# Attention in steps of 32 queries of eight heads, score products of 16 queries by 144 keys, gates by tanh, all engines in written order

## The chip, the cores and the metric

The kernel runs on one core of one Trainium2 chip. The core has a matrix engine (TensorE, PE in the profile; its weight loads stand apart as PEld), three engines for elementwise work (VectorE or DVE, ScalarE or ACT, GpSimd or POOL), and DMA queues that are fed by SyncE (SP), ScalarE and GpSimd. The metric is the time of one execution on the device, in microseconds; lower is better. Three runs of the kernel before took 806.92 to 807.62 us, with a median of 807.46 us.

## The reference, cut to what matters

One layer of a transformer trunk for 512 tokens of width 2048: a sliding-window attention with 32 query heads in 4 groups that share a key and a value head, a gate, an output projection, and then a gated embedding and a last norm. Of these, the attention and its gate are what the change rewrites:

```python
hn = rmsnorm(x, norm_g[i])
q, k, v, gate = jnp.split(h @ w_in, [SWA_WIDTH, SWA_WIDTH + SWA_KV_WIDTH, SWA_WIDTH + 2 * SWA_KV_WIDTH], axis=-1)
...
scores = jnp.einsum('bnqhgd,bnjhd->bnhgqj', q, kb).astype(jnp.float32) * (SWA_HEAD_DIM ** -0.5) + bias
scores = jnp.where(mask, scores, jnp.finfo(jnp.float32).min)
m = jnp.maximum(scores.max(axis=-1, keepdims=True), sink)
e = jnp.exp(scores - m)
probs = e / (e.sum(axis=-1, keepdims=True) + jnp.exp(sink - m))
out = jnp.einsum('bnhgqj,bnjhd->bnqhgd', probs.astype(vb.dtype), vb).reshape(bsz, seq, SWA_WIDTH)
return (out * jax.nn.silu(gate)) @ w_out
```

A query sees itself and the 127 keys before it. The bias depends on the distance alone; each head has a sink that joins the sum but has no value. Everything is float32.

## The kernel before

Every float32 product of the projections is made of three products of split operands (`mm3`: high by high, low by high, high by low). An operand is split by a ScalarE copy to the high part and a VectorE subtraction to the low part. The input weights come in pieces of 128 x 1024 (`wraw`), which `Weights` splits into `whi` and `wlo`; a piece serves eight k-steps, and one k-step is three matmuls of 512 columns. Thirty chunks of 128 columns are projected with 16 k-steps each: 14 query chunks (a chunk is two heads, a pair) and 16 gate chunks. Two further query pairs, the keys and the values are projected in the first stage, up to about 72 us.

Attention is 64 steps. Step i belongs to `d`, a group of two query pairs (four heads), and `g`, a block of 64 queries. `scores(i)` makes two products, one for each pair: the queries of the block and the two heads are the 128 stationary columns, and the keys move, 128 (first two blocks) or 192, twice, for the high and the low part of the key: 256 or 384 moving columns. VectorE adds bias and both halves (L392), folds the two ends of the window on one another (L407), and takes the maximum (L409); ScalarE makes the exponentials with their sum (L412) and multiplies by the inverse sum (L415). GpSimd writes the sink beside the scores (L388). `turn(i)` transposes the shares on PE and splits them into `r`; for later blocks GpSimd selects (L437) the triangle that belongs to the window's own end into `own`, and ScalarE copies the low part of `own` to the other half of the partitions (L444). `weigh(i)` multiplies `r` by the values and `own` by a difference of values `DV`, and every second step adds the output's halves (L470, L471) into `U`.

The loop over steps emits `turn(i - 2)`, `weigh(i - 3)`, `scores(i)` and then seven k-steps of the projection, which fill PE. PE, SP and POOL run in the order written; VectorE and ScalarE are ordered by the framework's scheduler. When a query chunk is done `evac_q` splits it from PSUM; a gate chunk is multiplied by `rb` (the inverse norm), and a silu runs over four chunks at once (L490), then `gate_value` multiplies by `U` (L485). Between steps `sum_weights` prepares sums of weight blocks in DRAM: SP copies a block, and GpSimd adds another by a DMA that accumulates (L536). These sums serve the two later stages, the output projection and the gated embedding, which multiply in seven products of blocks instead of eight. Their weights are split like the input's (L565, L566, `bhi` and `blo`).

The PSUM pool `p` has two banks for the projections, the scores have one buffer of two banks, the transposes (`t`) and the weighed outputs (`o`) two banks each.

## Time and profile before

| what | value |
|---|---|
| median of three runs | 807.46 us |
| span of the profiled execution | 805.0 us |
| PE busy | 791.9 us, 98% of the span |
| DVE busy | 583.7 us, 73% |
| ACT busy | 508.2 us, 63% |
| POOL busy | 111.1 us, 14% |
| mean granted clock of PE | 0.996 |
| first and last score product | 83.58 us and 442.78 us |

The profile is of one execution. Its page gives the span of the program's instructions; what lies around the span isn't profiled, and the page has no other time for that execution. PE's busy time counts pipelined matmuls, so it tells that PE rarely stood still, and the distance between starts tells what a matmul costs. An idle time names the engine and the line that ended it.

### The profile page before, as it was taken

To read this page: it belongs to the slowest core of one execution; us is meant where nothing else is said; L and a number is where in the kernel's file an instruction comes from. 1 tells how busy PE (TensorE), PEld (TensorE's weight loads), DVE (VectorE), ACT (ScalarE), POOL (GpSimd) and SP (SyncE) were. 2 spreads that over 40 slices of the span, in tenths; PEclk is the share of its full clock that TensorE was granted. 3 is DMA by queue.
4 is the path that set the end of the run, shared out by engine and by line. 5 is a ranking of instruction groups with operands and counts; after the bars stand their busy time and mean duration, and the time that the engine had idled before them with its cause. 6 is when DMAs were issued, how large, how long until landed. Compare 5 with 4: busy or idle time off the path is not lost.

```text
span 805.0 us, 10943 instructions
## 1 busy us (share of the span) xinstructions
PE 791.9 (98%) x3760; PEld 661.4 (82%) x3760; DVE 583.7 (73%) x953; ACT 508.2 (63%) x1036; POOL 111.1 (14%) x219
## 2 busy tenths in 40 slices
PE   9999999999999999999999999999999999999995
PEld 8888888878888888888888888888888888878884
DVE  4537776777767787776777898766646977879686
ACT  5635566676667786666586754555568756757545
POOL 0003113122121313122121100030000020200000
PEclk9999999999999999999999999999999999999998
DMA  8862877768697877867685459899612996876533
GB/s 336 310 173 52 250 241 197 221 185 230 149 259 209 198 230 189 223 182 218 178 210 141 120 215 356 307 293 249 201 53 85 376 204 202 167 199 206 181 106 105
DMA packets 45255, 165.15 MB, mean 205 GB/s; under 512 B 5952, under 2 KB 8128, under 8 KB 41360
## 3 DMA queue, kind: packets, MB, share of 16 engines
q1 hardware_dynamic: 38080, 130.20, 47.8%
q0 software_dynamic: 6832, 33.88, 22.6%
q8 instruction: 29, 0.48, 0.2%
q10 hardware_dynamic: 288, 0.39, 0.1%
q14 instruction: 26, 0.21, 0.1%
HBM read 158.63 MB, written 46.19 MB: 254 GB/s over the span
## 4 chain that ended last, share of the span: by engine, by line
PE 86%; issue 7%; DVE 2%; DMA 2%; POOL 1%; ACT 1%; SPq 0%; DVEq 0%; POOLq 0%; ACTq 0%
PE qps L122 7%; PE qps L121 7%; PE qps L120 7%; PE gps L121 7%; PE gps L122 7%; PE gps L120 7%; PE o L121 6%; PE o L120 6%; PE o L122 6%; PE s L383 2%; PE g L121 2%; PE g L122 2%; PE g L120 2%; PE o L461 2%; PE vps L229 2%
## 5 line engine op out<-in xcount | busy, mean ns | idle before, releaser
L566 DVE TENSOR_TENSOR blo<-braw,bhi 128x1024 fp32r<-128x1024 f32 x80 | 97.8, 1222 | 42.5 <-ACT bhi L565 42.4
L565 ACT CAST bhi<-braw 128x1024 fp32r<-128x1024 f32 x80 | 84.1, 1051 | 58.1 <-PE g L122 15.9
L122 PE MATMUL gps<-xh,wlo 128*128 128x512 f32 x256 | 100.1, 391 | 0.0
L121 PE MATMUL gps<-xl,whi 128*128 128x512 f32 x256 | 100.1, 391 | 0.0
L120 PE MATMUL gps<-xh,whi 128*128 128x512 f32 x256 | 99.9, 390 | 0.2 <-DVE q L266 0.2
L107 DVE TENSOR_TENSOR wlo<-wraw,whi 128x1024 fp32r<-128x1024 f32 x60 | 73.3, 1222 | 23.6 <-ACT whi L106 21.1
L122 PE MATMUL qps<-xh,wlo 128*128 128x512 f32 x224 | 87.8, 392 | 0.0
L121 PE MATMUL qps<-xl,whi 128*128 128x512 f32 x224 | 87.7, 391 | 0.0
L120 PE MATMUL o<-bhi,fho 128*128 128x512 f32 x224 | 87.7, 391 | 0.0
L122 PE MATMUL o<-bhi,flo 128*128 128x512 f32 x224 | 87.2, 389 | 0.0
L121 PE MATMUL o<-blo,fho 128*128 128x512 f32 x224 | 87.2, 389 | 0.0
L120 PE MATMUL qps<-xh,whi 128*128 128x512 f32 x224 | 87.2, 389 | 0.0
L412 ACT ACTIVATE t<-t,sm 128x129 f32<-128x129 f32 x128 | 50.6, 397 | 45.7 <-DVE sm L409 45.6
L106 ACT CAST whi<-wraw 128x1024 fp32r<-128x1024 f32 x60 | 62.9, 1048 | 24.8 <-PE gps L121 9.0
L121 PE MATMUL g<-blo,fhg 128*128 128x512 f32 x192 | 74.9, 390 | 0.6 <-DVE blo L566 0.6
L120 PE MATMUL g<-bhi,fhg 128*128 128x512 f32 x192 | 75.1, 391 | 0.0
L122 PE MATMUL g<-bhi,flg 128*128 128x512 f32 x192 | 74.8, 389 | 0.0
L437 POOL TENSOR_SCALAR_AFFINE_SELECT own<-r 64x512 fp32r<-64x512 f32 (+1 forms) x48 | 33.2, 691 | 298.2 <-DVE r L428 289.4
L122 PEld LDWEIGHTS gps<-xh,wlo 128*128 128x128 f32 x256 | 48.1, 188 | 10.2
L120 PEld LDWEIGHTS gps<-xh,whi 128*128 128x128 f32 x256 | 48.1, 188 | 9.4 <-PE vps L229 0.4
L121 PEld LDWEIGHTS gps<-xl,whi 128*128 128x128 f32 x256 | 48.1, 188 | 8.9
L566 DVE TENSOR_TENSOR blo<-grown,bhi 128x1024 fp32r<-128x1024 f32 x32 | 39.1, 1222 | 17.1 <-ACT bhi L565 17.1
(201 smaller groups left out, 1699.9 us busy)
## 6 DMA issues: line engine op xcount, KB each, us to landing
wraw<-in_w_gate_in SPq DMA_DIRECT2D x32, 512.0 KB, 5.7
wraw<-in_w_q SPq DMA_DIRECT2D x28, 512.0 KB, 4.6
w_out<-in_w_out POOLq DMA_DIRECT2D x24, 512.0 KB, 7.4
braw<-in_w_out SPq DMA_DIRECT2D x24, 512.0 KB, 4.1
braw<-in_ple_gate SPq DMA_DIRECT2D x24, 512.0 KB, 4.3
w_out<-in_w_out SPq DMA_DIRECT2D x16, 512.0 KB, 6.0
ple_gate<-in_ple_gate SPq DMA_DIRECT2D x16, 512.0 KB, 5.6
ple_gate<-in_ple_gate POOLq DMA_DIRECT2D x16, 512.0 KB, 7.1
```

What stands on the lines that cost most here:

```text
L106: nc.scalar.copy(hi, raw)
L107: nc.vector.tensor_sub(lo, raw, hi.bitcast(F32))
L120: nc.tensor.matmul(ps, sh, mh, start=first, stop=False, skip_group_check=more)
L121: nc.tensor.matmul(ps, sh, ml, start=False, stop=False, skip_group_check=more)
L122: nc.tensor.matmul(ps, sl, mh, start=False, stop=last, skip_group_check=more)
L229: nc.tensor.matmul(v_ps[t], h[:, c], both[:, :, 256:512], start=f, stop=e, skip_group_check=True)
L383: nc.tensor.matmul(s_ps[:, u, : 2 * n], st, key[:, :, first : first + n], start=True, stop=True)
L412: nc.scalar.activation(su, su, AF.Exp, bias=sm[:, u : u + 1], accum_out=sm[:, 2 + u : 3 + u])
L437: nc.gpsimd.affine_select(out=flat(own), in_=flat(r).bitcast(F32), pattern=[[0, 8], [sign, HB]], compare_op=ALU.is_ge, fill=0.0, base=-HB ...
L461: nc.tensor.matmul(out, first, r[:, low], start=low == 0, stop=own is None and low == 1)
L565: nc.scalar.copy(hi, raw)
L566: nc.vector.tensor_sub(lo, raw, hi.bitcast(F32))
```

## The change

Attention is cut in another way. A step now belongs to `kv`, a group of eight heads that share a key, and to 32 queries: two products of 16 queries by eight heads, again 128 stationary columns. The keys of 16 queries reach over 144 places and not 192, so 288 columns move; in the first block of 64 queries 64 keys (128 columns), in the second 128 (256 columns). There are still 64 steps of two products. The scale of the scores goes into the key, and the norm of the queries into `raw_q`, to which `evac_q` writes a chunk; `make_q` splits 128 queries of eight heads from there in four parts. The window's rest is masked by two memsets on GpSimd a step; the triangle is selected by two selects of 64 x 256, the second straight onto the other partitions, so the ScalarE copy of `own` goes. Bias and sinks have eight small loads each.

The gate is g(1 + tanh(g/2))/2: `evac_gate` multiplies by `rb`, writes tanh over the chunk in PSUM, a later VectorE operation (`rest`) closes it, and `gate_value` halves it as it multiplies by `U`. `gate_value`, `rest` and the splits of queries and keys wait in a list `fill`, from which a step takes two.

During attention all five engines run in written order. A step emits W.low for any open weight split, `turn`, `weigh`, `scores` and `place` (GpSimd's sink and masks), then `high`, `cross`, `shares` and the fill's ScalarE parts, `biased`, `low`, `merge` and the fill's VectorE parts, `exps`, W.high and `inverse`, and then the k-steps. Four heads' pairs must be ready before the first step, so the chunks come in another order, and 38 k-steps stand before the first scores, where 16 stood. The first twenty steps hold six k-steps each, the others seven.

The columns of PE first. The names are: `pt` the transposed shares, `o` the weighed output, `s` the scores, `k` and `q` key and queries, `qps` a projection's chunk. PE in a step early in attention, before:

```order
L122 MATMUL gps_1673<-xh_183,wlo_1546 128x512
L425 MATMUL pt_1687<-ident,t_1585 128x128 x2
L461 MATMUL o_1634<-r_1628,V_697 128x256 x2
L463 MATMUL o_1634<-own_1631,DV 128x256
L383 MATMUL s_1704<-k_701,q_1129 128x384
L383 MATMUL s_1704<-k_701,q_1262 128x384
L120 MATMUL gps_1673<-xh_214,whi_1545 128x512
L121 MATMUL gps_1673<-xl_215,whi_1545 128x512
```

The same place after:

```order
L126 MATMUL qps_2277<-xh_442,wlo_2260 128x512
L479 MATMUL pt_2348<-ident,t_2232 128x128 x2
L523 MATMUL o_2292<-r_2303,V_693 128x256 x2
L525 MATMUL o_2292<-own_2313,DV 128x256
L401 MATMUL s_2363<-k_1245,q_2120 128x288 x2
L124 MATMUL qps_2277<-xh_489,whi_2259 128x512
L125 MATMUL qps_2277<-xl_490,whi_2259 128x512
```

The two score products are of 288 columns and not 384.

VectorE in a step early in attention, before. `t` are the scores with the bias, `sm` the maxima, sums and inverses, `r` the transposed shares, `u` the output, `wlo` the low part of a weight piece, `rawq` the queries before their split:

```order
L392 SCALAR_TENSOR_TENSOR t_1166<-s_1163,sclq,bias_791 128x2x192
L392 SCALAR_TENSOR_TENSOR t_1166<-s_1163,sclq,t_1166 128x2x192
L407 TENSOR_TENSOR t_1166<-t_1166 128x2x64
L409 TENSOR_REDUCE sm_1171<-t_1166 128x2
L413 RECIPROCAL sm_1171<-sm_1171 128x2
L107 TENSOR_TENSOR wlo_1196<-wraw_1193,whi_1195 128x1024
L428 TENSOR_TENSOR r_1210<-pt_1207,r_1210 128x256
L471 TENSOR_TENSOR u_1030<-o_1159,tmp_1219 64x2x2x64
L392 SCALAR_TENSOR_TENSOR t_1227<-s_1224,sclq,bias_791 128x2x192
L471 TENSOR_TENSOR u_1030<-o_1159,tmp_1219 64x2x2x64
```

The same place after:

```order
L113 TENSOR_TENSOR wlo_1262<-wraw_1091,whi_1261 128x1024
L447 TENSOR_TENSOR t_1294<-s_1291,bias_788 128x2x144
L448 TENSOR_TENSOR t_1294<-s_1291,t_1294 128x2x144
L450 TENSOR_TENSOR t_1294<-t_1294 128x2x64
L452 TENSOR_REDUCE sm_1308<-t_1294 128x2
L492 TENSOR_TENSOR r_1298<-pt_1286,r_1298 128x256
L547 TENSOR_TENSOR u_1120<-o_1230,tmp_1300 64x4x4x16 x2
L465 RECIPROCAL sm_1308<-sm_1308 128x2
L257 TENSOR_TENSOR rawq_0_1053<-qps_1214,rb 128x256
L257 TENSOR_TENSOR rawq_1_1055<-qps_1214,rb 128x256
L113 TENSOR_TENSOR wlo_1321<-wraw_1147,whi_1320 128x1024
L447 TENSOR_TENSOR t_1356<-s_1353,bias_788 128x2x144
```

Before, the split `wlo` stood between the maximum and the inverse of the sums; now it stands behind the inverse, ahead of the next step's scores, and the low part `r` stands behind the maximum. The additions have 288 columns and the evacuation is two halves. ScalarE beside it, before:

```order
L412 ACTIVATE t_1166,sm_1171<-t_1166,sm_1171 128x129 x2
L106 CAST whi_1195<-wraw_1193 128x1024
L415 ACTIVATE t_1166<-t_1166,sm_1171 128x128 x2
L427 CAST r_1210<-pt_1207 128x256
L470 COPY tmp_1219<-o_1159 64x256 x2
L444 CAST own_1213<-own_1213 64x256
L412 ACTIVATE t_1227,sm_1232<-t_1227,sm_1232 128x129 x2
```

The same place after:

```order
L107 CAST whi_1261<-wraw_1091 128x1024
L484 CAST r_1298<-pt_1286 128x256
L538 COPY tmp_1300<-o_1230 64x256 x2
L471 ACTIVATE t_1236<-t_1236,sm_1251 128x128 x2
L461 ACTIVATE t_1294,sm_1308<-t_1294,sm_1308 128x129 x2
L107 CAST whi_1320<-wraw_1147 128x1024
```

Before, `whi` stood after or before the exponentials (the 128x129 rows) as the scheduler put it; now it always stands behind them. The copy of `own` is gone.

GpSimd in a step in the first half, before:

```order
L437 AFFINE_SELECT own_2583<-r_2580 128x512
L388 COPY t_2593<-sinkb 128x2
L536 DMA w_out_0_0_765<-in_w_out 64x2048
L437 AFFINE_SELECT own_2646<-r_2643 64x512
L388 COPY t_2660<-sinkb 128x2
L437 AFFINE_SELECT own_2706<-r_2703 128x512
L388 COPY t_2716<-sinkb 128x2
```

The same place after:

```order
L412 COPY t_2232<-sinkb 128x2
L420 MEMSET t_2232 128x16
L421 MEMSET t_2232 128x2x48
L503 AFFINE_SELECT own_2249<-r_2236 64x256 x2
L612 DMA w_out_0_3_757<-in_w_out 64x2048
L412 COPY t_2299<-sinkb 128x2
L418 MEMSET t_2299 128x2x48
L421 MEMSET t_2299 128x2x16
```

A step has two selects, one copy and two memsets where it had one select and one copy, around the same DMA that sums weights.

The diff, cut to its core:

```diff
+        def high(self):
+            i = len(self.made)
+            self.load(min(i + 3, len(self.srcs)))
+            hi, lo = (wpool.tile([P, WE], F32R, tag=f"w{v}", name=f"w{v}{i}") for v in ("hi", "lo"))
+            nc.scalar.copy(hi, self.raw[i])
+            self.made.append(tuple(t.rearrange("p (k c) -> p k c", k=8) for t in (hi, lo)))
+            self.open.append((lo, self.raw[i], hi))
+        def low(self):
+            lo, raw, hi = self.open.pop(0)
             nc.vector.tensor_sub(lo, raw, hi.bitcast(F32))
...
+    kinds, upto = [], {"q": 2, "g": 0}
+    for kind in "qq" + "qqqqggg" * (KVH - 1) + "ggggggg":
+        kinds.append((kind, upto[kind]))
+        upto[kind] += 1
...
+        kv, u = divmod(c, 4)
+        for n in range(2):
+            if u == 0:
+                raw_q[kv, n] = kvq.tile([P, 4, S // 2], F32, tag="rawq", name=f"rawq{kv}_{n}", bufs=3)
+            here = slice(n * (S // 2), (n + 1) * (S // 2))
+            nc.vector.tensor_mul(raw_q[kv, n][:, u], ps[:, here], rb[:, here])
+    def make_q(n, e, lo):
+        kv, b = divmod(n, NB)
+        if (e, lo) == (0, False):
+            Q[n] = kvq.tile([P, P // QB, GROUP, QB], F32R, tag="q", name=f"q{n}", bufs=2)
+        q = Q[n]
         halves = slice(0, 64), slice(64, 128)
...
+        src = raw_q[kv, b // 2][:, :, b % 2 * P : b % 2 * P + P].rearrange("p u (g q) -> p g u q", q=QB)
+        at = q.rearrange("p g (u e) q -> p g u e q", e=2)
+        if not lo:
+            nc.scalar.copy(at[halves[e], :, :, e], src[halves[e]])
+        else:
+            nc.vector.tensor_sub(at[halves[1 - e], :, :, e], src[halves[e]], at[halves[e], :, :, e].bitcast(F32))
...
+        for u in range(2):
+            st = q[:, (2 * i + u) % (P // QB)].rearrange("p h q -> p (h q)")
+            first = 0 if g < 2 else (g - 2) * HB + (s + u) * QB
+            nc.tensor.matmul(s_ps[:, u, : 2 * n], st, key[:, :, first : first + n], start=True, stop=True)
...
+    def place(i):
+        kv, j, g, s = where(i)
         odd = g % 2
...
+        n = (HB, P)[g] if g < 2 else P + QB
+        t = T[i] = apool.tile([P, 2, 4 + P + HB], F32, tag="t", name=f"t{i}", bufs=4)
         sink = 193 if odd else 0
...
+        nc.gpsimd.tensor_copy(t[:, :, sink], sinkb[:, kv : kv + 1].to_broadcast([P, 2]))
+        if g == 0:
+            nc.gpsimd.memset(t[:, :, 65:129], MASKED)
+        elif g >= 2:
+            fold = HB if odd or s else 2 * QB
+            if s:
+                nc.gpsimd.memset(t[:, :, 1 : 1 + (s + 1) * QB], MASKED)
+            else:
+                nc.gpsimd.memset(t[:, 1, 1 : 1 + QB], MASKED)
+            nc.gpsimd.memset(t[:, :, 1 + s * QB + n : 1 + P + fold], MASKED)
...
+            fold = HB if odd or s else 2 * QB
+            w = t.shape[-1]
+            at = 1 + s * QB
+            out = t[:, 0, at : at + n]
+            out = bass.AP(tensor=out.tensor, offset=out.offset, ap=[out.ap[0], [w + QB, 2], [1, n]])
+            nc.vector.tensor_add(out, s_ps[:, :, :n], bias[:, :n].unsqueeze(1).to_broadcast([P, 2, n]))
+            nc.vector.tensor_add(out, s_ps[:, :, n : 2 * n], out)
+            ends = t[:, :, 1 : 1 + fold], t[:, :, 129 : 129 + fold]
             nc.vector.tensor_max(ends[odd], ends[0], ends[1])
...
+        sm = SM[i] = apool.tile([P, 8], F32, tag="sm", name=f"sm{i}", bufs=4)
         nc.vector.tensor_reduce(sm[:, 0:2], seen, axis=AX.X, op=ALU.max, negate=True)
...
+            for low in range(2):
+                nc.gpsimd.affine_select(
+                    out=cols(own[places[g % 2 ^ low]]), in_=cols(r[here, low].bitcast(F32)),
+                    pattern=[[sign * QB, 2], [0, GROUP], [sign, QB]], compare_op=ALU.is_ge, fill=0.0,
+                    base=sign * s * QB - g % 2, channel_multiplier=-sign,
+                )
...
+        nc.vector.scalar_tensor_tensor(
+            out=src, in0=src, scalar=0.5, in1=U[c // 4][:, c % 4], op0=ALU.mult, op1=ALU.mult
+        )
+    def evac_gate(c, ps):
+        if c % 4 == 0:
+            gates[c // 4] = quarter(f"gate{c // 4}")
+        g = gates[c // 4][:, c % 4, :]
+        nc.vector.tensor_mul(g, ps, rb)
+        nc.scalar.activation(ps, g, AF.Tanh, scale=0.5)
+        def rest():
+            nc.vector.scalar_tensor_tensor(out=g, in0=ps, scalar=1.0, in1=g, op0=ALU.add, op1=ALU.mult)
             open_gates.add(c)
             if c in weighed:
                 due.append(c)
+        fill.append((None, rest))
...
     during = ExitStack()
     during.enter_context(
-        tc.manual_schedule(engines={getattr(mybir.EngineType, v) for v in ("PE", "SP", "Pool")})
+        tc.manual_schedule(
+            engines={getattr(mybir.EngineType, v) for v in ("PE", "SP", "Pool", "DVE", "Activation")}
+        )
     )
     load_bias(0)
-    for _ in range(KC):
-        next(proj)
-    blocks = TWOS * UNITS
-    left = KC * (len(kinds) - 1)
+    blocks = KVH * STEPS
+    at = 0
+    def ksteps(n):
+        nonlocal at
+        for _ in range(n):
+            while len(W.made) <= min(at // 8, len(W.srcs) - 1):
+                W.split()
+            at += 1
+            next(proj)
+    def splits(ahead):
+        return len(W.made) <= min(at // 8 + ahead, len(W.srcs) - 1)
+    for _ in range(2 * 2):
+        while splits(2):
+            W.split()
+        ksteps(8)
+    for e in range(2):
+        for lo in (False, True):
+            make_q(0, e, lo)
+    while splits(2):
+        W.split()
+    ksteps(6)
+    left = KC * len(kinds) - at
...
     for i in range(blocks + 3):
+        if i % 4 in (0, 1) and 4 <= i + 4 - i % 4 < blocks:
+            both(make_q, i // 4 + 1, i % 4)
+            fill.insert(0, fill.pop())
+        if i in (5, 20, 36):
+            both(make_key, 1 + i // 16)
+        if len(due) > sum(d is gate_value for _, d in fill):
+            fill.append((None, gate_value))
+        now = fill[:2]
+        del fill[:2]
+        while W.open:
+            W.low()
         if 2 <= i < blocks + 2:
             turn(i - 2)
         if 3 <= i:
             weigh(i - 3)
         if i < blocks:
             scores(i)
+            place(i)
+        if 2 <= i < blocks + 2:
+            high(i - 2)
+        if 3 <= i:
+            cross(i - 3)
+        if 1 <= i < blocks + 1:
+            shares(i - 1)
+        for act, dve in now:
+            if act:
+                act()
+        if i < blocks:
+            biased(i)
+        if 2 <= i < blocks + 2:
+            low(i - 2)
+        if 3 <= i:
+            merge(i - 3)
+        for act, dve in now:
+            dve()
+        if i < blocks:
+            exps(i)
             first_chores(i)
-            if i in (6, 20, 36):
-                make_key(1 + i // 16)
+        if splits(2):
+            W.high()
+        if i < blocks:
+            inverse(i)
         todo = left // (blocks + 2 - i) if i < blocks + 2 else 0
         left -= todo
-        for n in range(todo):
-            if n == 5 and due:
-                gate_value()
-            next(proj)
+        ksteps(todo)
         if i < blocks:
             for n in range(i * SUM_STEPS // blocks, (i + 1) * SUM_STEPS // blocks):
                 sum_weights(n)
+    while W.open:
+        W.low()
     for _ in proj:
         pass
+    while fill:
+        fill.pop(0)[1]()
...
-    nc = _bacc.Bacc("TRN2", target_bir_lowering=False, num_devices=1, dynamic_dma_scratch_size=8192)
+    nc = _bacc.Bacc("TRN2", target_bir_lowering=False, num_devices=1, dynamic_dma_scratch_size=4096)
```

More of the change, by code (lines that the diff above doesn't have):

```diff
@@ L99, in load, with split @@
                 nc.sync.dma_start(self.raw[i], self.srcs[i])
-        def _make(self, i):
-            self.load(i + 1)
-            raw = self.raw[i]
-            hi = wpool.tile([P, WE], F32R, tag="whi", name=f"whi{i}")
-            lo = wpool.tile([P, WE], F32R, tag="wlo", name=f"wlo{i}")
-            nc.scalar.copy(hi, raw)
-            nc.vector.tensor_sub(lo, raw, hi.bitcast(F32))
-            self.made.append(tuple(t.rearrange("p (k c) -> p k c", k=8) for t in (hi, lo)))
-        def get(self, i):
-            while len(self.made) <= min(i + self.ahead, len(self.srcs) - 1):
-                self._make(len(self.made))
-            return self.made[i]
-    W = Weights(ahead=2)
+        def high(self):
[7 more added lines that the diff above has]
+            lo, raw, hi = self.open.pop(0)
+            nc.vector.tensor_sub(lo, raw, hi.bitcast(F32))
+        def split(self):
+            self.high()
+            self.low()
+    W = Weights()
     def mm3(ps, sh, sl, mh, ml, first, last, more=False):
@@ L484, in gate_value @@
         src = gates[c // 4][:, c % 4, :]
-        nc.vector.tensor_mul(src, src, U[c // 2][:, c % 2])
-    def silu(g, some):
-        part = gates[g][:, some]
-        nc.scalar.activation(part, part, AF.Silu)
-        for c in range(4 * g + some.start, 4 * g + some.stop):
+        nc.vector.scalar_tensor_tensor(
+            out=src, in0=src, scalar=0.5, in1=U[c // 4][:, c % 4], op0=ALU.mult, op1=ALU.mult
[8 more added lines that the diff above has]
+            nc.vector.scalar_tensor_tensor(out=g, in0=ps, scalar=1.0, in1=g, op0=ALU.add, op1=ALU.mult)
             open_gates.add(c)
@@ L494, in silu @@
                 due.append(c)
+        fill.append((None, rest))
+    fill = []
     def blk(t):
```

222 lines of the change are left out of this document (106 added, 116 removed).

## The prediction

> **What bounds the kernel.** I read the busy table first, then the windows by stage, then who waited for whom on TensorE. The table's columns are busy time, share of the span and number of instructions.
>
> ```profile
> span 805.0 us, 10943 instructions
> ...
> PE 791.9 (98%) x3760; PEld 661.4 (82%) x3760; DVE 583.7 (73%) x953; ACT 508.2 (63%) x1036; POOL 111.1 (14%) x219
> ```
>
> The windows give busy time and instruction counts of PE, PEld, DVE, ACT and POOL, then granted clock, DMA share and GB/s. The first window lies inside attention, the second in the output projection just behind it.
>
> ```profile
> 120.00:160.00 40.00, 40.00 (x198) 33.57 (x197) 28.77 (x60) 26.12 (x75) 8.78 (x18) 1.00 0.73 210
> 460.00:480.00 20.00, 20.00 (x91) 16.60 (x90) 19.83 (x24) 12.35 (x17) 0.00 (x0) 1.00 0.57 209
> ```
>
> The waits of PE over the whole span, in us, times and longest, are small:
>
> ```profile
> PE o L463 <- ACT own L444: 1.5, 1, 1.5
> PE gps L120 <- DVE q L266: 0.2, 1, 0.2
> ```
>
> So TensorE is the bound at full clock, and it hardly ever waits. Only two things move the time: fewer matmul columns, and new or vanished waits of PE. The span is 805.0 us; the median of the runs is 807.46 us, so 2.5 us lie around the span, which I leave as they are. All sums below are differences, applied to the median.
>
> **Removed: score columns.** PE's timeline gives start and length. Lengths overlap, so the price of a matmul is the distance to the next start.
>
> ```profile
> 202.61 0.39 PE L120 MATMUL qps<-xh,whi 128*128 128x512 f32 x1
> ...
> 203.30 0.38 PE L425 MATMUL pt<-ident,t 128*128 128x128 f32 x2
> 203.44 0.48 PE L461 MATMUL o<-r,V 128*128 128x256 f32 x2
> 203.75 0.28 PE L463 MATMUL o<-own,DV 128*128 128x256 f32 x1
> 203.87 0.52 PE L383 MATMUL s<-k,q 128*128 128x384 f32 x2
> 204.22 0.39 PE L120 MATMUL qps<-xh,whi 128*128 128x512 f32 x1
> ...
> 209.61 0.51 PE L383 MATMUL s<-k,q 128*128 128x384 f32 x2
> ```
>
> ```profile
> 181.31 0.40 PE L383 MATMUL s<-k,q 128*128 128x256 f32 x2
> 181.55 0.40 PE L120 MATMUL gps<-xh,whi 128*128 128x512 f32 x1
> ```
>
> Two score products of 384 columns take 204.22 - 203.87 = 0.35 us, two of 256 take 0.24 us. That is 0.175 and 0.12 us each, or 0.43 ns a column, so 288 columns cost 0.12 + 32 x 0.43 ns = 0.134 us. Both kernels make 64 steps of two products. Of these 48 go from 384 to 288: 48 x 2 x 0.041 = 3.9 us. Of the other 16, eight stay at 256 and eight go to 128 columns; a 128-column transpose is 0.07 us ((203.44 - 203.30)/2), so 8 x 2 x 0.05 = 0.8 us. Together 4.7 us, all on PE's own path. A proportional price (288/384 of 0.175, and half of 0.12) would give 5.2 us; I take 4.7.
>
> The sustained spacing in the Trainium skill (TensorE: Matmul & The Clock Gate, Back-to-back issue gap) is about 81 ns at 128 columns and 131 ns at 512. By that slope of 0.13 ns a column the saving would be an estimated 1.5 us, and the sum 3.2 us smaller. The rows above disagree: 512 columns go at 0.23 us here, and the step from 384 to 256 costs 0.055 us a matmul, so the measurement decides.
>
> Transposes, weighing products and projections keep their number and size, and the heads' grouping adds no matmul.
>
> **Moved: projection before attention.** Four query pairs, not two, must be ready before a group of eight heads starts. So 38 k-steps of three matmuls stand before the first scores where 16 stood, and PE does no more work. But the first 20 attention steps now hold 6 k-steps instead of 7, the others 7. A k-step is (203.30 - 202.61) = 0.69 us, a step was 209.61 - 203.87 = 5.74 us. Less the 0.08 us of columns, steps become about 5.66 us, and the first twenty about 4.97 us. This shortens the time VectorE, ScalarE and GpSimd have for a step.
>
> **Removed: the silu and its table loads.** The one larger PE wait stands where a silu sits in ScalarE's queue:
>
> ```profile
> 174.89 1.28 ACT L490 ACT_TABLE_LOAD   x1
> 176.18 1.92 ACT L490 ACTIVATE gate<-gate 128x2048 f32<-128x2048 f32 x1
> ...
> 180.63 0.40 ACT L444 CAST own<-own 64x256 fp32r<-64x256 f32 x1 [0.75 <-POOL own L437]
> ```
>
> ```profile
> 178.54 0.36 PE L461 MATMUL o<-r,V 128*128 128x256 f32 x1
> ...
> 181.09 0.39 PE L463 MATMUL o<-own,DV 128*128 128x256 f32 x1 [1.49 <-ACT own L444]
> ```
>
> From 178.54 to 181.31 PE does what takes 0.43 us at 203.44: 2.3 us lost. In the new order tanh and exp share one load, and attention has one ACT_TABLE_LOAD where eight stood. Sixteen tanh of 128x512 replace five silu; a quarter of the 1.92 us silu with its fixed part is some 0.6 us each, so nothing of that length blocks the queue. I take 2.3 us; the bounds are 0 (another wait of that kind arises) and 2.3. The 0.2 us at the first projection goes too: the query evacuation is now one VectorE operation, without the ScalarE copy before it. Gain so far 4.7 + 2.3 + 0.2 = 7.2 us.
>
> **Added: work off PE.** Mean durations in attention, from the groups of the stretch 83 to 457 us (count, busy us, mean ns, then idle before):
>
> ```profile
> L107 DVE TENSOR_TENSOR wlo<-wraw,whi 128x1024 fp32r<-128x1024 f32 x57 | 69.6, 1222 | 18.9 <-ACT whi L106 16.5 <-PE s L383 1.7 <-PE pt L425 0.3
> L392 DVE SCALAR_TENSOR_TENSOR t<-s,sclq,t 128x384 f32<-128x384 f32 x48 | 29.6, 617 | 1.2
> L409 DVE TENSOR_REDUCE sm<-t 128x2 f32<-128x258 f32 x64 | 26.9, 420 | 7.2 <-POOL t L388 2.1 <-POOL t L398 0.8
> L428 DVE TENSOR_TENSOR r<-pt,r 128x256 fp32r<-128x256 f32 x64 | 26.8, 419 | 17.6 <-ACT r L427 16.9
> L471 DVE TENSOR_TENSOR u<-o,tmp 64x256 f32<-64x256 f32 x62 | 26.0, 419 | 1.9 <-ACT tmp L470 0.7
> L266 DVE TENSOR_TENSOR q<-qps,q 64x512 fp32r<-64x512 f32 x28 | 19.3, 689 | 4.2 <-ACT q L265 3.6
> L407 DVE TENSOR_TENSOR t<-t 128x128 f32<-128x128 f32 x48 | 14.1, 293 | 1.3
> L695 DVE TENSOR_TENSOR gate<-gps,rb 128x512 f32<-128x512 f32 x15 | 10.3, 686 | 3.5 <-PE gps L122 3.5
> ...
> L392 DVE SCALAR_TENSOR_TENSOR t<-s,sclq,t 128x256 f32<-128x256 f32 x8 | 3.8, 479 | 0.1
> ```
>
> VectorE saves about 0.16 us on each of 96 score additions (617 ns down to 419 + 32 x 1.08 ns = 454 ns; the slope is (617 - 479)/128), some 15 us. It adds 32 raw-query multiplications of 256 columns at 0.42 us (13 us) and 16 closing operations on the gates at about 0.7 us (11 us): 9 us more over 64 steps, 0.14 us a step. None of it is on PE's path by itself. ScalarE loses 48 copies of `own` and nine microseconds of table loads, and gets shorter.
>
> **The order as a loop.** What is late next is the chain that the written order makes inside a step: `biased` on VectorE, `exps` and then W.high on ScalarE, W.low on VectorE, then the next step's `biased`. The scheduler had put W.low beside the exponentials; now they follow each other.
>
> ```profile
> 446.20 0.40 ACT L412 ACTIVATE t<-t,sm 128x129 f32<-128x129 f32 x1 [0.90 <-DVE sm L409]
> ...
> 446.90 0.19 ACT L412 ACTIVATION_READ_ACCUMULATOR t<-t,sm 128x1 f32 x1
> ```
>
> ```profile
> L106 ACT CAST whi<-wraw 128x1024 fp32r<-128x1024 f32 x56 | 58.7, 1048 | 19.6 <-PE gps L121 9.0 <-PE qps L121 8.6 <-DMA wraw<-in_w_q 1.6
> ```
>
> `biased` is 2 x 0.454 + 0.293 + 0.420 = 1.62 us, with its three dependent starts about 1.75; `exps` are 446.20 to 447.09 = 0.89; W.high 1.05; W.low 1.22. The loop is 4.9 us with a split. A short step has a split in three of four (6 of 8 k-steps); without it VectorE alone has 1.75 + 0.42 + 0.42 (half of two merges) + 0.35 (half a query split) + 0.16 + 0.3 for evacuations = 3.4 us. The mean is (3 x 4.9 + 3.4)/4 = 4.5 us against 4.97. Steps that hold a merge, a query split and an evacuation together come to 5.8 us, so VectorE runs up to 2 us behind the scores and catches up again. PE's weighing product needs `low`, then the second select on POOL: 1.75 + 0.42 + some 0.4 = 2.6 us after `biased` starts, so PE waits once `biased` starts about 2 us late. That is just what the uneven steps reach. I put 0.1 us on each of the 20 short steps and 0.2 us on the joint of attention and output projection: 2.2 us. From below the cost is 0, since the means fit; from above 10 us, at half a microsecond on every short step.
>
> At the joint, two more gate products (four of 0.7 us, before two) and a closing operation stand ahead of the fourth weight split on VectorE, which is busy 19.83 of 20 us there while PE still does not wait. I count the 0.2 us.
>
> Edits priced at nothing: the 32 small bias loads and six more sink loads lie under the SP queue's loads, which run two splits ahead; if that cover goes, W.high comes late and the loop above pays. The smaller scratch for software DMA matters only with many sums under way; 40 sums in 64 steps of 5.7 us are 9 us apart, and one lands in 7.4:
>
> ```profile
> w_out<-in_w_out POOLq DMA_DIRECT2D x24, 512.0 KB, 7.4
> ```
>
> The key's scaling and the sink layout change no length on PE.
>
> Sum: 807.46 - 7.2 + 2.2 = 802.5 us.
>
> **Rivals.**
>
> 1. *The new order costs PE nothing.* The loop means (4.5 under 4.97 us, and 5.66 us later) speak for it, the 2 us lag against it. 800.3 us.
>
> 2. *A wait of the old kind stays*, at another place, and only the columns count: 807.46 - 4.9 + 2.2 = 804.8 us. For it speaks that such a wait was one event in 64 steps, so the trace shows little of its causes; against it that the loads that made it are gone.
>
> 3. *Fewer columns save nothing*, because the weight load bounds the spacing.
>
> ```profile
> L383 PEld LDWEIGHTS s<-k,q 128*128 128x128 f32 x128 | 19.9, 190 | 0.2
> ```
>
> A load takes 190 ns, longer than the 175 ns spacing. Then only 2.5 us come off: 807.46 - 2.5 + 2.2 = 807.2 us. Against it: products of 256 columns go at 0.12 us with the same loads.
>
> 4. *GpSimd closes the loop late, and it is slower.* POOL now makes two selects, a copy and two or three memsets a step, where it made one select and one copy, and its queue is in order with the sums' DMA issues:
>
> ```profile
> 320.40 1.22 DVE L107 TENSOR_TENSOR wlo<-wraw,whi 128x1024 fp32r<-128x1024 f32 x1
> ...
> 320.43 1.34 POOL L388 COPY t<-sinkb 128x2 f32<-128x2 f32 x2
> ```
>
> ```profile
> L437 POOL TENSOR_SCALAR_AFFINE_SELECT own<-r x48: 652/659/1584, 106.7 to 457.4; 64x512 fp32r<-64x512 f32 x24, 128x512 fp32r<-128x512 f32 x24
> ```
>
> Two copies took 1.34 us under a W.low; the select's median is 0.66 us and its longest 1.58 us. If the second select waits behind a query split (0.69) or a W.low (1.22), the weighing product comes that much later, and `biased` waits for the copy behind it. At 0.6 us on each short step and no more on long ones it costs 12 us: 807.46 - 7.2 + 12 = 812.3 us. It decides from 7.2/20 = 0.36 us a short step. Against it: most selects fall beside `merge`, and the long steps have 0.7 us more. In the Trainium skill (SBUF — State Buffer, Who interferes with whom) a VectorE instruction with two SBUF inputs and a GpSimd instruction that reads SBUF exclude each other; the two rows above agree, and the new query split reads two SBUF inputs where it read PSUM.
>
> **Chances.** Forecast 0.50 (its own range 801 to 804.5), rival 1 0.20, rival 2 0.10, rival 3 0.05, rival 4 0.15. A difference of 0.2%, 1.6 us, is about what can be told from no change here. Faster (under 805.8): 0.50 + 0.20 + 0.08 of rival 2 = 0.78. Same: the rest of rival 2, rival 3, 0.02 of rival 4 = 0.09. Slower: 0.13. The range 798.5 to 809.0 leaves out most of rival 4 and an edge below rival 1; its low end is 800.3 less 0.5 us by the proportional column price and 1.3 us for uncertainty of the vanished waits.
>
> **What would show it.** Right: the score group at 128x288 with a spacing near 0.134 us; steps between first score products of about 5.0, later 5.65 us; no PE wait near 2 us on `own`; one table load in attention; PE waits on POOL `own` or DVE `r` of 1 to 3 us in the first twenty steps. Wrong: PE waits repeated in long steps, a spacing of scores still near 0.17 us, POOL copies or selects above 1 us in most steps, or a wait on `blo` at the joint.

## The result, and the profile after

The changed kernel takes 798.82 us (median of 4 runs, 798.73 to 799.51), the kernel before 807.46 us beside it, the median of three executions; a fourth, of 1140.66 us, is left out of every figure here. The ratio is 0.9894, 95% interval 0.9879 to 0.9909: 1.06% faster. The profiled execution took 798.73 us, its span is 797.0 us, 8.0 us less than before. The forecast was 802.5 us in a range of 798.5 to 809.0: the sign and the range hold, the point is 3.7 us too high.

The busy table of the changed kernel, in the columns of the one shown of before:

```profile
span 797.0 us, 11130 instructions
...
PE 785.5 (99%) x3760; PEld 656.1 (82%) x3760; DVE 590.5 (74%) x1013; ACT 482.7 (61%) x992; POOL 149.6 (19%) x363
```

PE makes the same 3760 matmuls in 6.4 us less busy time. All its waits over the whole span (engine, what waited, what released it, us in total, times, longest):

```profile
PE warm_ps L145 <- PEq L1269: 0.8, 1, 0.8
PE g L125 <- DVE blo L642: 0.4, 1, 0.4
PE qps L216 <- ACT xh L199: 0.4, 1, 0.4
PE qps L126 <- DVE w0s L208: 0.2, 1, 0.2
PE o L525 <- POOL own L503: 0.2, 1, 0.2
```

Only the last row lies in the attention, at its very end. Before, the same list has six rows: beside the two that the prediction shows, 0.8, 0.6 and 0.4 us outside attention and 0.3 us for `r` right behind the silu. The 1.5 us wait for the copy of `own` is gone, and in the 64 steps nothing took its place. The score products, on PE's timeline (start, length, operation, count):

```profile
211.40 0.28 PE L525 MATMUL o<-own,DV 128*128 128x256 f32 x1
211.52 0.43 PE L401 MATMUL s<-k,q 128*128 128x288 f32 x2
211.79 0.40 PE L124 MATMUL qps<-xh,whi 128*128 128x512 f32 x1
...
217.17 0.43 PE L401 MATMUL s<-k,q 128*128 128x288 f32 x2
```

Two products of 288 columns take 211.79 - 211.52 = 0.27 us, 0.135 us each as forecast (0.134), and a long step is 217.17 - 211.52 = 5.65 us. ScalarE's table loads in the attention, from its groups there (count, busy us, mean ns):

```profile
L571 ACT ACTIVATE gps<-gate 128x512 f32<-128x512 f32 x16 | 9.6, 602 | 13.3 <-DVE gate L570 13.3
L461 ACT ACT_TABLE_LOAD x1 | 1.3, 1283 | 0.0
```

One load is left, and a tanh of 128x512 takes 0.602 us, as the 0.6 us reckoned. Where the 8.0 us of span lie, by the first matmul of each stage:

| stretch | before | after | difference |
|---|---|---|---|
| start to the first matmul of the later projection | 72.60 | 71.80 | -0.80 |
| projection and attention, to the output projection | 387.78 | 380.72 | -7.06 |
| output projection | 157.71 | 157.76 | +0.05 |
| gated embedding to the end | 186.94 | 186.74 | -0.20 |

### The profile page after: what moved, and what is told of

It is laid out like the page before. It is cut to its first block, busy times and chain, and to the rows that moved or that the text cites. A ratio compares the mean times of both kernels' runs of the same rounds, so it can differ in the third digit from the quotient of the medians.

```text
span 797.0 us, 11130 instructions
## 1 busy us (share of the span) xinstructions
PE 785.5 (99%) x3760; PEld 656.1 (82%) x3760; DVE 590.5 (74%) x1013; ACT 482.7 (61%) x992; POOL 149.6 (19%) x363
## 4 chain that ended last, share of the span: by engine, by line
PE 85%; issue 7%; DMA 3%; DVE 3%; POOL 1%; ACT 1%; SPq 0%; DVEq 0%; POOLq 0%; ACTq 0%
PE qps L126 7%; PE qps L124 7%; PE qps L125 7%; PE gps L124 7%; PE gps L125 7%; PE gps L126 7%; PE o L124 6%; PE o L126 6%; PE o L125 6%; PE s L401 2%; PE g L125 2%; PE g L126 2%; PE g L124 2%; PE o L523 2%; PE vps L228 2%
## 5 line engine op out<-in xcount | busy, mean ns | idle before, releaser
L503 POOL TENSOR_SCALAR_AFFINE_SELECT own<-r 64x256 fp32r<-64x256 f32 x96 | 61.2, 637 | 193.0 <-ACT r L484 109.3
L484 ACT CAST r<-pt 128x256 fp32r<-128x256 f32 x64 | 23.8, 372 | 55.4 <-PE pt L479 55.1
```

What stands on the lines that cost most here:

```text
L484: nc.scalar.copy(r[:, 0], PT[i])
L503: nc.gpsimd.affine_select(out=cols(own[places[g % 2 ^ low]]), in_=cols(r[here, low].bitcast(F32)), pattern=[[sign * QB, 2], [0, GROUP], [s ...
```

## The experiments

The main theory was the prediction's: columns and the vanished wait pay, and the written order takes a part back in the short steps, since its loop of VectorE and ScalarE is nearly as long as they are. The main rival: the order costs nothing. The first four runs take one part each.

**1. The columns alone.**

```diff
-        n = (HB, P)[g] if g < 2 else P + QB
+        n = P if g < 2 else P + HB
+        first = max(g - 2, 0) * HB
...
```

The rest of the edit makes VectorE read the same 144 of the 192 places; its rows keep their shape and length.

> The changed kernel with score products as wide as before (192 keys or, in the first two blocks, 128), of which the extra columns are not read; everything else is as changed. If the columns are worth what the spacing of the rows says (0.041 us for each of 96 products, 0.05 to 0.06 us for each of 16), it is 4.5 to 5.2 us slower than the changed kernel: about 803.6 us. If the weight loads bound the spacing, it is within 0.5 us of it, and the gain came from elsewhere. If VectorE were the bound, it would be within 0.5 us too.

Measured: 804.71 us (803.34 to 806.01), ratio to before 0.9963 (0.9951 to 0.9974); span 803.5 us. Its score products, and the next matmul behind them:

```profile
213.40 0.51 PE L401 MATMUL s<-k,q 128*128 128x384 f32 x2
213.75 0.39 PE L124 MATMUL qps<-xh,whi 128*128 128x512 f32 x1
```

The pair takes 0.35 us again instead of 0.27. The 63 distances between one step's scores and the next add up to 342.52 us, in the changed kernel to 338.25 us: 4.3 us are the columns' worth on PE's path. The other 2.2 us of the 6.5 us of span are not in the steps: 0.5 us lie before the projection, 1.3 us in the output projection (0.6 us of them a wait of PE for `blo`) and 0.4 us behind it. The rival by which fewer columns save nothing is out: a weight load of 190 ns does not bound the spacing.

**2. The written order of two engines.** PE, SP and GpSimd keep the order; VectorE and ScalarE go back to the scheduler.

```diff
-            engines={getattr(mybir.EngineType, v) for v in ("PE", "SP", "Pool", "DVE", "Activation")}
+            engines={getattr(mybir.EngineType, v) for v in ("PE", "SP", "Pool")}
```

> The changed kernel with VectorE and ScalarE left to the scheduler during attention, as in the kernel before. If the written order gives nothing and costs nothing, within 1 us of the changed kernel (798 to 800 us). If the written order is what keeps PE from waiting, PE waits of 1 to 3 us come back and it is 801 to 806 us. If the written order costs PE time, it is faster by up to 0.5 us, which is all that is left of PE waits in attention.

Measured: 798.39 us (798.24 to 798.93), ratio to before 0.9886 (0.9866 to 0.9905). The rows of both engines stand in another order, and yet every attention step has the changed kernel's length to 0.02 us. At the joint PE has no wait, and from the last scores to the output projection it takes 16.15 us where the changed kernel takes 16.61. So the written order of these engines costs 0.46 us at the joint and nothing in the steps, and it gives nothing: the 2.0 us that the forecast put on the short steps are not there.

**3. Tanh in the kernel before.**

```diff
-                        nc.vector.tensor_mul(gates[g][:, c % 4, :], ps, rb)
-                        if g == 3 and c % 4 >= 2:
-                            silu(g, slice(0, 3) if c % 4 == 2 else slice(3, 4))
-                        elif c % 4 == 3:
-                            silu(g, slice(0, 4))
+                        part = gates[g][:, c % 4, :]
+                        nc.vector.tensor_mul(part, ps, rb)
+                        nc.scalar.activation(ps, part, AF.Tanh, scale=0.5)
+                        nc.vector.scalar_tensor_tensor(
+                            out=part, in0=ps, scalar=1.0, in1=part, op0=ALU.add, op1=ALU.mult
+                        )
...
```

> The kernel before with the gate's silu replaced by tanh and a closing VectorE operation, chunk by chunk, and nothing else. If the silu and its table loads made the one PE wait of 2.3 us, that wait is gone and it takes 805.0 to 805.5 us against 807.5. If the scheduler's order made the wait whatever the function, a wait of 1 to 3 us stays somewhere and it is 806.5 to 808 us.

Measured: 804.86 us (804.02 to 805.49), ratio 0.9962 (0.9950 to 0.9974), span 802.8 us: 2.2 us off the span. The step of 7.94 us became 5.61 us, and PE has no wait between 83 and 458 us. These 2.3 us came from how the gates were opened.

**4. One more reduction on VectorE in each step.**

```diff
+        nc.vector.tensor_reduce(sm[:, 6:8], seen, axis=AX.X, op=ALU.max, negate=True)
```

> The changed kernel with the maximum of each step taken twice (a second reduction of 0.42 us that nobody uses, ahead of the exponentials), so that the loop of biased, exponentials and weight split is 0.42 us longer in every step. By the prediction's loop (4.5 us mean and 2 us of lag under 4.97) the short steps are then full and PE loses 1 to 5 us: 800 to 804 us. If the loop has more room than was worked out, it costs under 0.5 us: 798.8 to 799.3 us. If the loop already bounds the steps, 20 to 64 steps times 0.42 us: 807 us and more.

Measured: 801.34 us (801.17 to 802.99), span +2.5 us. All of it lies in the first twenty steps (2.4 us together, the other 43 distances agree to 0.01), and 1.42 us in one, the seventh. There the changed kernel still has room. Ahead of the product with `own` at 130.62 stand, on its timeline:

```profile
124.22 1.39 DVE L295 TENSOR_TENSOR k<-kt,k 64x512 fp32r<-64x512 f32 x2
...
125.72 1.21 DVE L113 TENSOR_TENSOR wlo<-wraw,whi 128x1024 fp32r<-128x1024 f32 x1
...
126.84 0.45 DVE L447 TENSOR_TENSOR t<-s,bias 128x288 f32<-128x288 f32 x1
...
128.49 0.41 DVE L492 TENSOR_TENSOR r<-pt,r 128x256 fp32r<-128x256 f32 x1
...
129.04 0.51 POOL L503 TENSOR_SCALAR_AFFINE_SELECT own<-r 64x256 fp32r<-64x256 f32 x1 [1.73 <-DVE r L492]
...
130.62 0.28 PE L525 MATMUL o<-own,DV 128*128 128x256 f32 x1
```

The split of a key (1.39) and of a weight (1.21) hold VectorE up, `biased` starts at 126.84, 1.0 us behind its scores (125.81), and the select still ends at 129.55, 1.07 us before PE needs it. One step later the lag is at its longest in the twenty short steps and the room at its shortest, 132.17 - 130.74 = 1.43 us behind the scores and 0.7 us before the product:

```profile
132.17 0.45 DVE L447 TENSOR_TENSOR t<-s,bias 128x288 f32<-128x288 f32 x1
...
134.36 0.51 POOL L503 TENSOR_SCALAR_AFFINE_SELECT own<-r 64x256 fp32r<-64x256 f32 x1 [1.75 <-DVE r L492]
...
135.59 0.28 PE L525 MATMUL o<-own,DV 128*128 128x256 f32 x1
```

With 0.4 us more in each step, the lag reaches PE, most in the seventh:

```profile
130.77 0.41 DVE L494 TENSOR_TENSOR r<-pt,r 128x256 fp32r<-128x256 f32 x1
131.24 0.38 PE L525 MATMUL o<-r,V 128*128 128x256 f32 x1 [0.64 <-DVE r L494]
131.32 0.51 POOL L505 TENSOR_SCALAR_AFFINE_SELECT own<-r 64x256 fp32r<-64x256 f32 x1 [3.48 <-DVE r L494]
131.88 0.39 PE L527 MATMUL o<-own,DV 128*128 128x256 f32 x1 [0.26 <-POOL own L505]
```

So the waits are of the kind that the prediction named, `r` and `own` in crowded short steps, but they begin only beyond the load of this change.

**5. The same extra reduction, with short and long steps mixed.**

```diff
-        todo = left // (blocks + 2 - i) if i < blocks + 2 else 0
-        left -= todo
+        todo = left * (i + 1) // (blocks + 2) - left * i // (blocks + 2) if i < blocks + 2 else 0
...
+        nc.vector.tensor_reduce(sm[:, 6:8], seen, axis=AX.X, op=ALU.max, negate=True)
```

> The extra reduction of one_reduce_more stays (0.42 us a step on VectorE), but the 6-k-step and 7-k-step attention steps are now mixed evenly, where the twenty short ones stood in a row at the start. The projection's work is the same in number and only moves by a step or so. Theory A (VectorE's lag piles up over a row of short steps, so 2.5 us were lost there): with long steps of 5.65 us between, the lag is caught up, the time is 798.8 to 799.8 us, and no attention step is more than 0.3 us longer than its k-steps make it. Theory B (the 2.5 us come from single crowded steps, such as the sixth, which holds the scaling of a key, whatever the steps beside it): about 801 us again, with one step about 1.4 us too long.

Measured: 799.72 us (799.47 to 800.10). From the first scores to the last it takes 338.6 us, 0.3 us more than the changed kernel with no extra reduction, and that 0.3 us lies in one step. Theory A holds: it is the row of short steps, over which VectorE's lag adds up, not the crowded step as such.

**6. and 7. Two more reductions, in the written order and in the scheduler's.** The edit of run 4, made twice; run 7 has the edit of run 2 as well.

> Two extra reductions in each attention step, results unused, 0.84 us a step on VectorE between the scores and the exponentials. Theory A (the loop through VectorE and ScalarE, as the prediction reckoned it: a step with a split 4.9 us, plus 0.84, three in four short steps hold one, so a mean of 5.35 us against 4.94): PE loses about 0.4 us on each of some 18 short steps, 7 us and more with the lag of the crowded ones; the long steps (5.55 against 5.62 us) hardly lose: 806 to 810 us. Theory B (each reduction costs the same 2.5 us as the first, in crowded steps alone): 803.8 us. Theory C (the loop is longer than reckoned, and long steps lose too): 0.2 us on each of 44 long steps more, above 815 us.

> two_reduces_more (815.5 us, 16.6 us over the changed kernel) with VectorE's and ScalarE's rows left to the scheduler during attention, as in scheduler_order; PE, SP and GpSimd keep the written order. Theory A (the written order makes the tight loop: W.low follows the exponentials and W.high inside a step, where the scheduler may set it beside them): VectorE's work of a step then fits beside ScalarE's, and most of the 16 us come back: 799 to 806 us. Theory B (it is the amount of work and its data dependences, not the order in which the two engines take it): 812 to 818 us. Theory C (the scheduler, which plans by costs of its own, puts rows that PE needs late once there is little room): above 818 us.

Measured: 815.46 us (815.28 to 815.78) in the written order, 800.12 us (799.22 to 801.07) in the scheduler's. In the written order the short steps lose 9.6 us and, against my reckoning, the long ones 6.5 us, nearly all of it in eight of them, up to 1.5 us in one. The time is worse than theory A's and at theory C's edge. PE's waits over the whole span:

```profile
PE o L527 <- POOL own L505: 5.5, 15, 0.7
PE o L525 <- DVE r L494: 3.6, 6, 1.2
```

In the scheduler's order every step is again as long as in the changed kernel to 0.02 us, with VectorE busy 89.9 of 99 us. What the rows show to differ is where the low half of the transposed weights (`r`, which PE waits for) stands. In the written order it is behind the whole of `biased`, with the extra reductions in it:

```profile
120.85 0.46 DVE L448 TENSOR_TENSOR t<-s,t 128x288 f32<-128x288 f32 x1
121.34 0.23 DVE L450 TENSOR_TENSOR t<-t 128x64 f32<-128x64 f32 x1
121.61 0.42 DVE L452 TENSOR_REDUCE sm<-t 128x2 f32<-128x258 f32 x1
121.94 0.87 DVE L454 TENSOR_REDUCE sm<-t 128x2 f32<-128x258 f32 x2
122.73 0.41 DVE L494 TENSOR_TENSOR r<-pt,r 128x256 fp32r<-128x256 f32 x1
123.20 0.38 PE L525 MATMUL o<-r,V 128*128 128x256 f32 x1 [0.70 <-DVE r L494]
```

The scheduler sets it in 30 of 62 steps between two pieces of `biased`:

```profile
152.91 0.45 DVE L448 TENSOR_TENSOR t<-s,t 128x288 f32<-128x288 f32 x1
153.28 0.42 DVE L494 TENSOR_TENSOR r<-pt,r 128x256 fp32r<-128x256 f32 x1
153.61 0.29 DVE L450 TENSOR_TENSOR t<-t 128x128 f32<-128x128 f32 x1
```

In every step of the scheduler's order `r` is ready at least 0.9 us before PE needs it, in the written order in several only 0.05 us before. So the waits belong to the written order and not to the amount of work. That the place of `r` makes them is read from these rows; no run moves that row alone. The loop through ScalarE that the prediction reckoned shows as well: from 97 to 196 us VectorE waits 4.2 us for `whi` in the written order and 1.1 us in the scheduler's. In this change the lag stays short of what PE would notice.

**8. GpSimd's selects made twice.**

```diff
-            for low in range(2):
+            for low in (0, 0, 1, 1):
                 nc.gpsimd.affine_select(
```

> Each of GpSimd's two selects on the weights of the pair block is made twice, so GpSimd has four of 0.5 us in 48 of 64 steps where it had two. Theory A (the order has room: in the fullest short step the select after W.low ended 1.07 us before PE needed it, at 129.55 against 130.62 us): only the joint to the output projection, where PE waited 0.36 us for this select, gets 0.5 us longer: 799.2 to 800 us. Theory B (the prediction's rival 4, GpSimd closes the loop late once it is a little slower): 0.3 us or more on each short step with a select, 803 us or more, with waits of PE or VectorE for GpSimd in the trace.

Measured: 801.45 us (801.03 to 803.68), span +2.2 us. In the steps PE loses 0.3 us in all, and 1.7 us more lie between the last scores and the output projection, where theory A had 0.5 us:

```profile
451.10 2.62 DVE L734 TENSOR_TENSOR gate<-gate 128x1024 f32<-128x1024 f32 x2
451.25 2.84 POOL L503 TENSOR_SCALAR_AFFINE_SELECT own<-r 64x256 fp32r<-64x256 f32 x2 [2.04 <-DVE r L492]
...
454.14 0.39 PE L525 MATMUL o<-own,DV 128*128 128x256 f32 x1 [1.88 <-POOL own L503]
```

Two selects take 2.84 us there, beside subtractions of two SBUF operands on VectorE. The same place in the changed kernel:

```profile
450.67 2.62 DVE L734 TENSOR_TENSOR gate<-gate 128x1024 f32<-128x1024 f32 x2
450.81 1.43 POOL L503 TENSOR_SCALAR_AFFINE_SELECT own<-r 64x256 fp32r<-64x256 f32 x1 [2.65 <-DVE r L492]
...
452.30 0.38 PE L525 MATMUL o<-own,DV 128*128 128x256 f32 x1 [0.20 <-POOL own L503]
```

The one select takes 1.43 us instead of some 0.5, and PE starts about 0.4 us late: by this reckoning it would not have waited without the 0.9 us. The slow select alone is not enough. Run 2 has it too, beside the same rows and without a wait, since the split of `r` began 2.51 us before PE's products with it and not 1.38:

```profile
449.39 2.62 DVE L734 TENSOR_TENSOR gate<-gate 128x1024 f32<-128x1024 f32 x2
449.54 1.43 POOL L503 TENSOR_SCALAR_AFFINE_SELECT own<-r 64x256 fp32r<-64x256 f32 x1 [1.45 <-DVE r L492]
...
451.80 0.28 PE L525 MATMUL o<-own,DV 128*128 128x256 f32 x1
```

GpSimd does not close the loop in the steps, even with twice the selects: rival 4 is out.

**9. and 10. Silu, or its length?** The changed kernel with silu instead of tanh, and the kernel before with one silu for each chunk.

```diff
-        nc.scalar.activation(ps, g, AF.Tanh, scale=0.5)
+        nc.scalar.activation(ps, g, AF.Silu)
-            nc.vector.scalar_tensor_tensor(out=g, in0=ps, scalar=1.0, in1=g, op0=ALU.add, op1=ALU.mult)
+            nc.vector.tensor_copy(g, ps)
...
```

> The written order stays, but the sixteen gate chunks are opened by silu instead of tanh (the closing operation becomes a copy, of the same 128x512 on VectorE, and the scale by 0.5 goes). Silu and the exponentials do not share a table here, so up to 32 loads of 1.28 us return to ScalarE, two around each chunk, in the chain of exponentials and W.high. Theory A (what the prediction named as the cause of the 2.3 us wait: loads in the queue ahead of what PE needs): about 2.6 us more in each of 16 steps, of which the step's room (0.7 to 1 us between loop and PE) hides a part: 1.5 us each, some 24 us, so 815 to 830 us. Theory B (ScalarE is busy only 61% and has room for 41 us; only the old order, not the loads, made the wait): 798.8 to 801 us.

Measured: 801.42 us (800.86 to 802.09), far below theory A and 0.4 us above theory B. ScalarE's groups in the attention:

```profile
L461 ACT ACT_TABLE_LOAD x15 | 19.2, 1283 | 2.5 <-DVE sm L452 2.2
L571 ACT ACT_TABLE_LOAD x15 | 19.2, 1283 | 0.3
```

Thirty loads, 38 us of ScalarE, cost the attention's steps 0.1 us. The loss lies later: 1.8 us between the last scores and the output projection (1.1 us of them a wait for `own` at the joint), 0.9 us in that projection and 0.3 us behind it.

```diff
-                        if g == 3 and c % 4 >= 2:
-                            silu(g, slice(0, 3) if c % 4 == 2 else slice(3, 4))
-                        elif c % 4 == 3:
-                            silu(g, slice(0, 4))
+                        silu(g, slice(c % 4, c % 4 + 1))
```

> The kernel before, with its silu still a silu, but each gate chunk opened by its own activation of 128x512 (0.60 us in silu_in_order) as soon as it is there, sixteen instead of five of up to 128x2048 (1.92 us). The scheduler's order stays, and up to 32 table loads of 1.28 us stand in attention where eight stood. Theory A (the length of the lump, 1.28 + 1.92 us in one piece, made the 2.3 us wait; loads with a short activation fit into ScalarE's idle time, as silu_in_order showed for the written order): the wait is gone and the time is that of before_with_tanh, 804 to 806 us. Theory B (the loads themselves, in an order that the scheduler chose without knowing them): the wait comes back at several chunks, 808 us or more, with PE waits of 1 us or more on own or r.

Measured: 805.90 us (804.10 to 806.44), ratio 0.9980 (0.9969 to 0.9991). With 28 loads instead of eight the 7.94 us step is gone (5.61 us); one other step is 0.23 us longer than in run 3. The interval overlaps that of run 3. So the number of loads did not make PE wait; it took a long piece, load and silu of 128x2048 together 3.2 us in ScalarE's queue. The length alone is not enough either: in the kernel before the same piece stands at 280.61 and 411.23 us and PE does not wait. The first one stood ahead of the copy of `r` that PE needed next (178.00), the one at 411.23 right behind the copy of `own`. And the select behind the first took 1.37 us, where its median is 0.66.

## Why the prediction came out as it did

| term | forecast, us | measured, us | from |
|---|---|---|---|
| score columns | -4.7 | -4.3 | steps, run 1 against the changed kernel |
| wait behind the silu | -2.3 | -2.3 | the step of 7.94 us, 5.61 in run 3 |
| wait at the first projection | -0.2 | -0.3 | from the matmul before it 0.23 us, before 0.56 |
| twenty short steps, 0.1 us each | +2.0 | 0.0 | steps, run 2 |
| joint to the output projection | +0.2 | +0.5 | 16.61 us against 16.15 in run 2 |
| not in the sum | 0 | -2.2 | below |

The measured column adds up to 798.82 - 807.46 = -8.6 us; its last row is what the others leave.

- **What failed is the term "0.1 us on each of the 20 short steps".** Its mechanism is right in the place and in the rows that PE would wait for, as runs 4 to 7 show. Its size is not. I let PE wait "once `biased` starts about 2 us late", and expected that lag to be reached. The 2 us were about right: in the seventh and eighth step lag and room left add up to 2.1 us each (1.03 and 1.07, 1.43 and 0.7). But 1.43 us is the longest lag in the twenty steps. The forecast's own mean, 4.5 us against 4.97, had said so; I added a wait for a peak that is not reached. Rival 1, 800.3 us, was the better case. That the measured time lies in the range, 0.3 us above its low end, is in part luck: 2.2 us of the gain were in no term.
- **Columns.** 0.04 us for each of 96 products is right; they gave 4.2 of the 4.3 us. The narrowest steps gave nearly nothing: the two first distances are 4.31 and 4.45 us with 128 columns and 4.34 and 4.48 with 256, the other six differ by 0.01 us, 0.1 us together where I had 0.8. In the seventeenth step the next matmul starts 0.18 us after the pair of 128 columns and 0.24 us after that of 256, but then takes 0.28 us to the one behind it instead of 0.23. So for these the distance to the next start was not the price.
- **The silu.** The size is right (2.3 us by run 3). The prediction named both causes in one breath, table loads and the long piece; run 10 shows that it took the long piece, and the two later pieces that it also took a bad place.
- **The joint** is a slow select behind a late `r`, not the weight split that I had counted on. In the changed kernel PE did not wait for the fourth split there.
- **Not in the sum, 2.2 us.** Three steps of before, 5.94 us long where their neighbours have 5.73, became ordinary (0.6 us; the row of waits did not show them). In each, ScalarE's copy of `own`, which the change removes, ended 0.05 us before the product began, here 220.60 + 0.40 against 221.05:

```profile
220.60 0.40 ACT L444 CAST own<-own 64x256 fp32r<-64x256 f32 x1 [2.80 <-POOL own L437]
...
221.05 0.39 PE L463 MATMUL o<-own,DV 128*128 128x256 f32 x1
```

The start up to the projection is 0.5 us shorter beyond the wait counted, and that differs from one execution to the next: the first key product begins at 6.24 to 7.28 us in nine executions with the new start and at 6.67 to 7.30 us in three with the old one, and from there to the projection both take 65.0 us, but for the wait counted and stalls of 0.2 to 0.8 us that come with both. Another 0.5 us lie in the rest of the span, without a cause. The last 0.6 us lie around it (807.46 - 805.0 = 2.5 us before, 798.82 - 797.0 = 1.8 us now), but the 2.5 us set the median beside the span of another execution: of 44 later executions of the kernel before 41 took 1.76 to 2.09 us more than their span.
- **Rival 2** (a wait of the old kind stays) did not come: no wait stands in the steps.

No run beats the changed kernel by more than the measurement tells; run 2 is 0.05% below it. It has the larger reserve, as run 7 shows.

## What to carry to other kernels

Before a wait is charged for a loop that nearly fills its step, find the fullest step and reckon when the consumer needs the result; a lag that the consumer never sees costs nothing. How near the edge is can be measured in one run, by adding a known amount of unused work to the loop. A written order without loss may still have less reserve than a scheduled one, since each row waits for all rows written ahead of it; the rows of runs 6 and 7 suggest that, where an engine serves two consumers, the row that the bound engine waits for should go first. For a queue in order, the longest single piece, and what stands behind it, counts more than the sum of the pieces.

## What was not expected of the hardware

The select on GpSimd depends little on its size and much on its neighbour. Its row for the changed kernel (count, min, median and max in ns):

```profile
L503 POOL TENSOR_SCALAR_AFFINE_SELECT own<-r x96: 497/504/1595, 126.2 to 450.8; 64x256 fp32r<-64x256 f32 x96
```

A quarter to a half of the elements of before takes 504 ns where those took 659. The longest stands beside a weight split on VectorE:

```profile
131.02 1.59 POOL L503 TENSOR_SCALAR_AFFINE_SELECT own<-r 64x256 fp32r<-64x256 f32 x1 [1.05 <-ACT r L484]
131.03 1.22 DVE L113 TENSOR_TENSOR wlo<-wraw,whi 128x1024 fp32r<-128x1024 f32 x1
```

That is 1.09 us more than its median, nearly the whole of the split's 1.22 us. It is no single case: all 22 of the 96 selects above 0.7 us overlap a VectorE instruction with two SBUF inputs by 0.47 us or more, the other 74 by 0.24 us at most. The rule cited in the prediction, from the Trainium skill (SBUF — State Buffer, Who interferes with whom), that a VectorE instruction with two SBUF inputs and a GpSimd instruction which reads SBUF exclude each other, agrees with this pair, with these counts, and with the 1.43 and 2.84 us at the joint.
